# Token norms of a two-block transformer forward: ScalarE scales the tokens, plain transposes, per-feature shift and scale at the emptying of the banks, a shorter reciprocal root

## The chip, the cores and the metric

The kernel runs on one core of a Trainium2 chip. The metric is the device time of one execution in microseconds (us), as the median of several runs. The engines of a core work side by side, each through its own list of instructions in order, and wait for each other by semaphores: TensorE (PE, matrix products, with its weight loads shown as PEld), VectorE (DVE), ScalarE (ACT), GpSimd (POOL) and SyncE (SP, which here only starts DMAs).

## The reference, cut to what matters

256 tokens of 1024 features pass through two blocks. Everything is float32. The norms are these:

```python
def rms_norm(x, g):
    return x * lax.rsqrt(jnp.mean(x * x, -1, keepdims=True) + 1e-6) * g

def layer_norm(x, g, b):
    mu = jnp.mean(x, -1, keepdims=True)
    var = jnp.mean(jnp.square(x - mu), -1, keepdims=True)
    return (x - mu) * lax.rsqrt(var + 1e-5) * g + b

def first_block(x, ...):
    x = even_layer(x, ...)      # x + (forgetting and dilated attention of rms_norm(x)) @ w_out
    x = odd_layer(x, ...)       # x + (retention of rms_norm(x), group norm by head) @ w_out
    return rms_norm(x, final_norm)

def second_block(x, ...):
    h = layer_norm(x, ln_in_g, ln_in_b)
    for l in range(2):
        m = hybrid_mixer(h, ...)                       # compressed, selected, window attention, convolution
        h = layer_norm(ALPHA * h + m, ln1_g[l], ln1_b[l])
        f = swiglu(h, ...) if l == 0 else moe_swiglu(h, ...)   # dense FFN; 8 experts, top 2
        h = layer_norm(ALPHA * h + f, ln2_g[l], ln2_b[l])
    return h
```

## The kernel before, in words

The residual stream `x` lies in SBUF as two token tiles of 128 tokens by 1024 features (tile 0 and tile 1). Each layer multiplies the normed tokens by weights. The operand of those products is `xT`, the normed tokens transposed (features on the partitions), held as two parts, a high and a low one (`xT_129` and `xT_130` in the rows). One product of float32 quality is made of three matmuls of such parts, `mm3` (L181 to L183). The weights stream from HBM through SP's DMA queue (L42) into five buffers `w_raw`; ScalarE splits off the high part `w_hi` (L56) and VectorE the low part `w_lo` (L58), into four buffers each.

A layer ends in `out_units`, whose results are added to `x`. The last four pairs of weight chunks are run for tile 0 first (48 matmuls of 128x512), then `done(0, ...)` is called, then the same 48 for tile 1. `done(tt, ...)` is the norm of one tile: add the result to `x`, statistics, reciprocal root, transposes into `xT`. The next layer opens with `token_units`: 72 matmuls of 128x256 that need only tile 0, then `late`, which is `done(1, ...)`, then 72 that need tile 1. So each norm of tile 0 has tile 1's 48 matmuls to lie beside, and each norm of tile 1 the next layer's 72 matmuls of tile 0 (ahead of the MoE layer there are none: its router needs the norm first). Where an instruction stands in its engine's list is decided when the program is built, by a scheduler that takes the instructions in the order of the code unless it reckons that another is ready earlier; PE then runs its list strictly in order.

The boundaries with such a norm are six: the setup at the start (both tiles, nothing beside it), even to odd layer (both with `rms`), odd layer to mixer 0, mixer 0 to FFN, FFN to mixer 1 and mixer 1 to MoE (all with `layer_norm`, in short LN). A last norm, with no transposes, writes the output.

Before, the factor r of a token (the reciprocal root) is put into the transposing matmul: `diagonal` writes r on the diagonal of a 128x128 matrix `dr` (L397), and the matmul of `x` with `dr` (L411, float32, 8 for a tile, recorded as 16 passes) transposes and scales at once. For LN, VectorE has before that written (y - mean) * g over `x` (L381, two instructions of 128x512), and the shift b comes from a matmul of 24 rows in bf16 ahead of each bank's transposes (L407, two for a tile). The bank is emptied in two pieces of 128x512 by ScalarE (L429, high part) and VectorE (L431, low part); with `rms`, in 8 pieces of 128x128 each, which also apply the scale by feature (L419, L423). `update` later completes `x` itself as x * r + b (L389 on VectorE; for the MoE layer ScalarE L386 and GpSimd L387). `rsqrt` (L311 to L321) is 9 small VectorE instructions for one variance: a first guess by integer arithmetic and three Newton steps of two.

```python
t.matmul(out, l[0], r[0], start=start, stop=False, skip_group_check=True)   # L181
...
self.nc.tensor.matmul(ps[:, k, :], src[:, d], dr[:], start=shift is None, stop=True,   # L411
```

Of the kernel before, what the change touches and what calls it, by code (L numbers as in the profile page):

```python
# [119 lines left out]
class Stack:  # L120
# [34 lines left out]
    def load_shifts(self):  # L155
        for g in range(2):
            for j in range(3):
                p = 64 * g + 8 * j
                self.nc.gpsimd.dma_start(self.xs[p:p + 8, 1, 0:256].rearrange("p (i f) -> p i f", i=2),
                                         self.a["shifts"][2 * g:2 * g + 2].rearrange("i c f -> c i f"))  # L160

    def split_shifts(self):

        v = self.nc.vector
        for g in range(2):
            r = slice(64 * g, 64 * g + 24)
            t, f = self.shifts[r].rearrange("p i f -> p (i f)"), self.xs[r, 1, 0:256]
            v.tensor_copy(self.chunk[r], self.pick[r, 0:8])
            for j in range(2):
                v.tensor_copy(t, f)  # L170
                v.scalar_tensor_tensor(f, t, self.pick[r, 8 + j:9 + j], f, op0=ALU.mult, op1=ALU.add)
            v.tensor_copy(t, f)

    def shift(self, i):
        r = slice(64 * (i // 2), 64 * (i // 2) + 24)
        return self.shifts[r, i % 2], self.chunk[r]

# [128 lines left out]
    def rsqrt(self, mul, eps, *var):  # L306

        v = self.nc.vector
        xyt = [[self.small(1, "rs_" + n) for n in "xyt"] for _ in var]
        for (x, y, t), a in zip(xyt, var):  # L310
            v.tensor_scalar(x[:], a, 0.5 * mul, 0.5 * eps, op0=ALU.mult, op1=ALU.add)  # L311
        for x, y, t in xyt:
            v.tensor_single_scalar(y[:].bitcast(I32), x[:].bitcast(I32), 1, op=ALU.logical_shift_right)
        for x, y, t in xyt:
            yi = y[:].bitcast(I32)
            v.tensor_scalar(yi, yi, -1, 0x5f3759df - (1 << 22) - (1 << 31), op0=ALU.mult, op1=ALU.add)
        for _ in range(3):
            for x, y, t in xyt:
                v.scalar_tensor_tensor(t[:], y[:], y[:], x[:], op0=ALU.mult, op1=ALU.mult)  # L319
            for x, y, t in xyt:  # L320
                v.scalar_tensor_tensor(y[:], t[:], 1.5, y[:], op0=ALU.subtract, op1=ALU.mult)  # L321
        return [y[:] for _, y, _ in xyt]
# [19 lines left out]
    def rms(self, g, accs, between=0):  # L342

        ds = []
# [8 lines left out]
        for (tt, _), r in zip(accs, ds):  # L353
            ins = self.transpose(tt, self.x[:, tt], r, scale=g)
        return ins

    def layer_norm(self, tt, g, b, bT=None, acc=None, rms=None):

# [14 lines left out]
        if rms is None:  # L373
            r, = self.rsqrt(1.0, 1e-5, mv[:, 1:2])
        else:
# [3 lines left out]
            r, = self.rsqrt(1.0, 0.0, mv[:, 1:2])  # L379
# [10 lines left out]
        if bT is None:  # L390
            return update()
# [1065 lines left out]
```

## Time and profile before

| | |
|---|---|
| median of 3 runs | 1412.96 us (1412.95 to 1418.4) |
| the profiled execution | 1414.13 us, span 1412.4 us, so 1.7 us lie around the span |
| mean granted clock of PE | 0.99 of full |
| busy share of the span | PE 97%, DVE 78%, ACT 59%, POOL 7% |
| moved from HBM | 298.79 MB, mean 212 GB/s |

PE is busy for nearly the whole span, so a reader looks first for the few places where it is not, and asks at each which engine's work ends last. The rows that a profile prints give a start, a duration, the engine, the line, and what an instruction writes and reads. Matmuls overlap in PE's pipeline, so what one costs is read from the distance between two starts, not from its duration.

### The profile page before, as it was taken

The page shows a single profiled execution, that of the slowest core. Times are in us where ns is not written, and L with a number is a line of the kernel's source. Part 1 is how long each engine was busy: PE and PEld are TensorE (multiplying, and loading weights), DVE is VectorE, ACT ScalarE, POOL GpSimd, SP SyncE. Part 2 cuts the span into 40 slices and gives each one's busy share as a digit, 9 for nine tenths or more (in the row PEclk, how much of TensorE's full clock was granted, in tenths as well). Part 3 has the DMA queues.
Part 4 walks back from the last instruction along what each step waited for, and adds up shares of the span by engine and source line. Part 5 has one row for each costly group of instructions (what it writes and reads, how often), then busy time and mean ns, then how long its engine had stood idle before and what let it go on. Part 6 is the DMA issues. An engine that isn't in the chain of part 4 may idle for free. (4 is left out here: it accounts for less than half of the span.)

```text
span 1412.4 us, 24934 instructions
## 1 busy us (share of the span) xinstructions
PE 1367.0 (97%) x9907; PEld 1268.7 (90%) x9907; DVE 1101.9 (78%) x2013; ACT 836.0 (59%) x1394; POOL 102.5 (7%) x141
## 2 busy tenths in 40 slices
PE   7999999999999999999999999998999999999994
PEld 7999999799999898979998798977999999999983
DVE  7867666577777679887655479978989989989987
ACT  7666666364545357634444247744777777777762
POOL 2000000000000100010000000013010110120110
PEclk9999999999999999999999999998999999999997
DMA  8644444354444365436555455324989889889882
GB/s 299 236 150 150 150 151 150 119 205 176 173 156 165 99 252 200 146 124 225 181 187 197 151 197 207 121 99 145 365 319 352 320 324 349 305 320 348 328 326 76
DMA packets 45389, 301.58 MB, mean 214 GB/s; under 512 B 6016, under 2 KB 6256, under 8 KB 10576
## 3 DMA queue, kind: packets, MB, share of 16 engines
q1 hardware_dynamic: 42192, 293.20, 56.3%
q0 software_dynamic: 2928, 6.69, 1.7%
q8 instruction: 80, 1.31, 0.4%
q14 instruction: 45, 0.37, 0.1%
q10 hardware_dynamic: 144, 0.01, 0.0%
HBM read 298.79 MB, written 1.05 MB: 212 GB/s over the span
## 5 line engine op out<-in xcount | busy, mean ns | idle before, releaser
L58 DVE TENSOR_TENSOR w_lo<-w_raw,w_hi 128x1024 fp32r<-128x1024 f32 x553 | 673.0, 1248 | 157.3 <-ACT w_hi L56 156.5
L56 ACT ACTIVATE w_hi<-w_raw 128x1024 fp32r<-128x1024 f32 x553 | 560.9, 1055 | 217.2 <-PE ps L183 103.6
L181 PE MATMUL ps<-xT,w_hi 128*128 128x256 f32 x1072 | 304.5, 284 | 0.0
L183 PE MATMUL ps<-xT,w_lo 128*128 128x256 f32 x1072 | 301.3, 281 | 0.0
L182 PE MATMUL ps<-xT,w_hi 128*128 128x256 f32 x1072 | 301.1, 281 | 0.0
L181 PEld LDWEIGHTS ps<-xT,w_hi 128*128 128x128 f32 x1072 | 201.9, 188 | 2.8 <-issue 2.6
L183 PEld LDWEIGHTS ps<-xT,w_lo 128*128 128x128 f32 x1072 | 202.0, 188 | 0.3 <-issue 0.3
L182 PEld LDWEIGHTS ps<-xT,w_hi 128*128 128x128 f32 x1072 | 202.0, 188 | 0.0
L182 PE MATMUL ps<-w_lo,xe 128*128 128x256 f32 x704 | 199.3, 283 | 1.2 <-DVE w_lo L58 1.1
L181 PE MATMUL ps<-w_hi,xe 128*128 128x256 f32 x704 | 198.9, 283 | 0.0
L183 PE MATMUL ps<-w_hi,xe 128*128 128x256 f32 x704 | 198.8, 282 | 0.0
L181 PE MATMUL ps<-w_hi,xT 128*128 128x256 f32 x528 | 148.5, 282 | 0.0
L182 PE MATMUL ps<-w_lo,xT 128*128 128x256 f32 x528 | 147.7, 280 | 0.0
L183 PE MATMUL ps<-w_hi,xT 128*128 128x256 f32 x528 | 146.6, 279 | 0.0
L182 PEld LDWEIGHTS ps<-w_lo,xe 128*128 128x128 f32 x704 | 132.5, 188 | 2.9 <-DVE w_lo L58 2.2
L181 PEld LDWEIGHTS ps<-w_hi,xe 128*128 128x128 f32 x704 | 132.9, 189 | 0.6
L183 PEld LDWEIGHTS ps<-w_hi,xe 128*128 128x128 f32 x704 | 132.6, 188 | 0.0
L181 PEld LDWEIGHTS ps<-w_hi,xT 128*128 128x128 f32 x528 | 99.9, 189 | 0.3
L182 PEld LDWEIGHTS ps<-w_lo,xT 128*128 128x128 f32 x528 | 99.8, 189 | 0.3
L183 PEld LDWEIGHTS ps<-w_hi,xT 128*128 128x128 f32 x528 | 99.0, 188 | 0.1
L1232 POOL TENSOR_TENSOR x<-x,part 128x512 f32<-128x512 f32 x28 | 47.3, 1722 | 335.7 <-ACT part L1228 274.7
L465 ACT ACTIVATE P<-P,sm_mx 128x128 f32<-128x128 f32 (+1 forms) x128 | 56.9, 446 | 23.4 <-DVE sm_mx L461 23.1
(358 smaller groups left out, 2176.5 us busy)
## 6 DMA issues: line engine op xcount, KB each, us to landing
w_raw<-in_wts SPq DMA_DIRECT2D x271, 1024.0 KB, 4.9
w_raw<-in_wth SPq DMA_DIRECT2D x11, 512.0 KB, 3.6
w_raw<-in_ln_g POOLq DMA_DIRECT2D x3, 512.0 KB, 4.2
w_raw<-in_ln_b POOLq DMA_DIRECT2D x3, 512.0 KB, 5.4
x<-in_x SPq DMA_DIRECT2D x4, 256.0 KB, 3.8
out<-x SPq DMA_DIRECT2D x4, 256.0 KB, 2.1
dec<-in_dec POOLq DMA_DIRECT2D x1, 512.0 KB, 9.0
w_raw<-in_final_norm POOLq DMA_DIRECT2D x1, 512.0 KB, 4.0
```

The source lines that it names most:

```text
L56: self.nc.scalar.activation(hi[:, d], t[:, d], AF.Copy)
L58: self.nc.vector.tensor_sub(lo[:, d], t[:, d], hi[:, d].bitcast(F32))
L181: t.matmul(out, l[0], r[0], start=start, stop=False, skip_group_check=True)
L182: t.matmul(out, l[0], r[1], start=False, stop=False, skip_group_check=True)
L183: t.matmul(out, l[1], r[0], start=False, stop=stop, skip_group_check=True)
L465: s.activation(p[:, h, :], p[:, h, :], AF.Exp, bias=mx[:, o + h:o + h + 1], scale=-1.0, accum_out=rs[:, o + h:o + h + 1])
L1232: nc.gpsimd.tensor_add(x, x, t[:])
```

## The change

The factor r no longer goes through the matmul. With `rms`, ScalarE writes x * r into a second buffer (two of 128x512 for a tile, `to`), with LN it writes (y - mean) * r over `x` (bias -mean * r, a new small VectorE instruction, `ln_mr`), and VectorE then multiplies by g (two of 128x512). The transposes are plain ones by the identity. The shift b by feature is added where the bank is emptied, which for LN too is now done in 8 pieces of 128x128 by ScalarE (bias) and 8 by VectorE. `update` has only b left to add. The matmuls of the shifts, the six DMAs that loaded them and the VectorE work that split them are gone; one DMA brings a table of them in float32. `rsqrt` still has 9 instructions for a variance, made another way (the guess in one, a step of four and a step of three), and takes two variances in one set, which the group norm of the odd layer uses.

```diff
-    def rsqrt(self, mul, eps, *var):
+    def rsqrt(self, mul, eps, var):
         v = self.nc.vector
...
+        x, y, t = (self.small(2, "rs_" + n)[:, 0:var.shape[1]] for n in "xyt")
+        k = (1024 / 27) ** 2
+        v.tensor_scalar(x, var, k * mul, k * eps, op0=ALU.mult, op1=ALU.add)
+        v.tensor_scalar(y.bitcast(I32), x.bitcast(I32), -0.5, float(0x5f3759df - (1 << 31)), op0=ALU.mult, op1=ALU.add)
+        v.tensor_mul(t, y, y)
+        v.tensor_mul(t, t, x)
+        v.scalar_tensor_tensor(t, t, 10 / 3, t, op0=ALU.subtract, op1=ALU.mult)
+        v.scalar_tensor_tensor(y, t, 5.0, y, op0=ALU.add, op1=ALU.mult)
+        v.tensor_mul(t, y, y)
+        v.tensor_mul(t, t, x)
+        self.last = v.scalar_tensor_tensor(y, t, 64 / 3, y, op0=ALU.subtract, op1=ALU.mult)
+        return y
...
-    def rms(self, g, accs, between=0):
+    def rms(self, g, accs, to, between=0):
...
-            r, = self.rsqrt(1.0 / D, 1e-6, ms[:])
-            ds.append(self.diagonal(r))
+            r = self.rsqrt(1.0 / D, 1e-6, ms[:])
+            for d in self.halves():
+                self.acted = self.nc.scalar.activation(to[:, tt, d], self.x[:, tt, d], AF.Copy, scale=r)
...
-            ins = self.transpose(tt, self.x[:, tt], r, scale=g)
+            ins = self.transpose(tt, to[:, tt], scale=g)
...
+        mr = self.small(1, "ln_mr")
+        v.scalar_tensor_tensor(mr[:], mv[:, 0:1], -1.0, r, op0=ALU.mult, op1=ALU.mult)
         for d in self.halves():
-            v.scalar_tensor_tensor(xs[:, d], y[:, d], mv[:, 0:1], g[:, d], op0=ALU.subtract, op1=ALU.mult)
+            self.acted = self.nc.scalar.activation(xs[:, d], y[:, d], AF.Identity, bias=mr[:], scale=r)
+        for d in self.halves():
+            self.last = v.tensor_mul(xs[:, d], xs[:, d], g[:, d])
         def update(spread=False):
             for d in self.halves():
-                if spread:
-                    self.nc.scalar.activation(xs[:, d], xs[:, d], AF.Copy, scale=r)
-                    self.nc.gpsimd.tensor_add(xs[:, d], xs[:, d], b[:, d])
-                else:
-                    v.scalar_tensor_tensor(xs[:, d], xs[:, d], r, b[:, d], op0=ALU.mult, op1=ALU.add)
+                (self.nc.gpsimd if spread else v).tensor_add(xs[:, d], xs[:, d], b[:, d])
...
-    def diagonal(self, r):
-        dr = self.sm.tile([128, 128], F32, name="dr", bufs=2)
-        self.last = self.nc.vector.tensor_scalar(dr[:], self.ident, r, None, op0=ALU.mult)
-        return dr
...
-            if shift is not None:
-                rows, chunk = shift
-                self.nc.tensor.matmul(ps[:], rows, chunk[:, 4 * n:4 * n + 4, None].to_broadcast([24, 4, 128]),
-                                      start=True, stop=False, skip_group_check=True)
             for k in range(4):
                 d = slice((4 * n + k) * 128, (4 * n + k + 1) * 128)
-                self.nc.tensor.matmul(ps[:, k, :], src[:, d], dr[:], start=shift is None, stop=True,
-                                      skip_group_check=True)
-            if scale is None:
-                ins = self.split_into(self.xT[0][:, 4 * n:4 * n + 4, t], self.xT[1][:, 4 * n:4 * n + 4, t], ps[:])
-                continue
+                self.nc.tensor.transpose(ps[:, k, :], src[:, d], self.ident)
             for k in range(4):
                 c = 4 * n + k
                 hi, lo = (x[:, c, t] for x in self.xT)
-                self.nc.scalar.activation(hi, ps[:, k], AF.Copy, scale=scale[:, c:c + 1])
+                if scale is None:
+                    self.nc.scalar.activation(hi, ps[:, k], AF.Identity, bias=shift[:, c:c + 1])
+                else:
+                    self.nc.scalar.activation(hi, ps[:, k], AF.Copy, scale=scale[:, c:c + 1])
             for k in range(4):
...
-                ins = self.nc.vector.scalar_tensor_tensor(lo, ps[:, k], scale[:, c:c + 1], hi.bitcast(F32), op0=ALU.mult,
+                f, op = (shift, ALU.add) if scale is None else (scale, ALU.mult)
+                ins = self.nc.vector.scalar_tensor_tensor(lo, ps[:, k], f[:, c:c + 1], hi.bitcast(F32), op0=op,
                                                           op1=ALU.subtract)
...
+        nc.gpsimd.dma_start(self.shifts[:], a["shifts"])
...
+            to = self.spare()
+            nc.gpsimd.memset(to[:, :, 0:1], 0.0)
```

The instructions also come to stand in other places. On PE, at the end of mixer 0, the list before runs as follows where tile 0's matmuls end and tile 1's begin (`ps` are the accumulators, `yc` and `q` the operands of the output product):

```order
L181 MATMUL ps_6985<-w_hi_6996,q0_5588 128x512
L182 MATMUL ps_6985<-w_lo_6997,q0_5588 128x512
L183 MATMUL ps_6985<-w_hi_6996,q1_5589 128x512
L407 LDWEIGHTS shifts_132
L407 MATMUL ps_7083<-chunk_131,shifts_132 128x512
L181 MATMUL ps_6986<-w_hi_6711,yc0_5586 128x512
L182 MATMUL ps_6986<-w_lo_6712,yc0_5586 128x512
L183 MATMUL ps_6986<-w_hi_6711,yc1_5587 128x512
```

`ps_6985` belongs to tile 0 and `ps_6986` to tile 1; between them stands only one matmul of the shifts. Then, after 21 matmuls of tile 1, the transposes of tile 0's norm:

```order
L181 MATMUL ps_6986<-w_hi_6854,yc0_5586 128x512
L182 MATMUL ps_6986<-w_lo_6855,yc0_5586 128x512
L183 MATMUL ps_6986<-w_hi_6854,yc1_5587 128x512
L411 MATMUL ps_7075<-dr_7073,x_111 128x128 x4
L411 MATMUL ps_7083<-dr_7073,x_111 128x128 x4
L181 MATMUL ps_6987<-w_hi_6854,yc0_5586 128x512
```

The list of the change at the same end of mixer 0 (`mm3` is L158 to L160 there, the transposes are L383, `cst` is the identity; `ps_6933` is tile 0's, `ps_6934` and `ps_6935` are tile 1's):

```order
L158 MATMUL ps_6933<-w_hi_6944,q0_5524 128x512
L159 MATMUL ps_6933<-w_lo_6945,q0_5524 128x512
L160 MATMUL ps_6933<-w_hi_6944,q1_5525 128x512
L383 MATMUL ps_7025<-cst_113,x_111 128x128 x4
L383 MATMUL ps_7038<-cst_113,x_111 128x128 x4
L158 MATMUL ps_6934<-w_hi_6659,yc0_5522 128x512
L159 MATMUL ps_6934<-w_lo_6660,yc0_5522 128x512
L160 MATMUL ps_6934<-w_hi_6659,yc1_5523 128x512
L158 MATMUL ps_6935<-w_hi_6659,yc0_5522 128x512
```

The transposes of tile 0 moved from behind 21 of tile 1's 48 matmuls to directly behind tile 0's last matmul, ahead of all 48. The end of mixer 1 reads the same: 5721 `mm3` matmuls of the program stood ahead of its first tile-0 transpose, and 5700 do now, of which the last is tile 0's last. At the other three boundaries the count moves by 2 to 4 matmuls only (even to odd 1697 to 1700, odd to mixer 0 3134 to 3136, FFN to mixer 1 5084 to 5088), and for tile 1's transposes not at all, at any of them.

On VectorE, the norm of tile 1 at the end of mixer 0 now stands like this, from its statistics on (`x` is the token tile, `ps` the transposes' bank, L368 the product with g, L372 the update, L395 the emptying):

```order
L294 SCALAR_TENSOR_TENSOR rs_y<-rs_t,rs_y 128x1
L295 TENSOR_TENSOR rs_t<-rs_y 128x1
L296 TENSOR_TENSOR rs_t<-rs_t,rs_x 128x1
L297 SCALAR_TENSOR_TENSOR rs_y<-rs_t,rs_y 128x1
L364 SCALAR_TENSOR_TENSOR ln_mr<-ln_mv,rs_y 128x1
L368 TENSOR_TENSOR x<-x,w_raw 128x512 x2
L372 TENSOR_TENSOR x<-x,w_raw 128x512 x2
L395 SCALAR_TENSOR_TENSOR xT_132<-ps,shifts,xT_131 128x128 x8
```

Before, the two `update` instructions (L389) alternated with the two that empty a bank (L431), one of each in turn; now both stand ahead of all eight pieces (L395).

## Rows read from the trace of the kernel before

**Rows 1.** The page's first part: busy time, share of the span, instructions of each engine.
```profile
PE 1367.0 (97%) x9907; PEld 1268.7 (90%) x9907; DVE 1101.9 (78%) x2013; ACT 836.0 (59%) x1394; POOL 102.5 (7%) x141
```
**Rows 2.** Waits of PE: total us, times, longest us.
```profile
PE ps L411 <- DVE dr L397: 13.8, 3, 8.9
```
**Rows 3.** Timeline of PE (start us, us, engine, line, op): transposes by either kind of matmul.
```profile
299.98 1.95 PE L411 MATMUL ps<-dr,x 128*128 128x128 f32 x16
301.69 0.37 PE L181 MATMUL ps<-w_hi,xT 128*128 128x256 f32 x1
...
1010.40 1.36 PE L1192 MATMUL ps<-cst,he 128*128 128x128 f32 x11
1011.52 0.37 PE L181 MATMUL ps<-w_hi,xe 128*128 128x256 f32 x1
```
**Rows 4.** Timeline, end of mixer 0: tile 0's last matmul to its transposes.
```profile
615.88 0.40 PE L183 MATMUL ps<-w_hi,q 128*128 128x512 f32 x1
...
616.53 0.50 PE L181 MATMUL ps<-w_hi,yc 128*128 128x512 f32 x1
...
616.87 0.39 PE L182 MATMUL ps<-w_lo,yc 128*128 128x512 f32 x1
617.10 0.39 PE L183 MATMUL ps<-w_hi,yc 128*128 128x512 f32 x1
...
617.77 0.21 DVE L372 BATCH_NORM_AGGREGATE ln_mv<-ln_st 128x2 f32<-128x12 f32 x1
...
621.54 1.95 PE L411 MATMUL ps<-dr,x 128*128 128x128 f32 x16
```
**Rows 5.** Timelines of ACT and DVE: pieces of the norms.
```profile
948.20 0.71 ACT L386 ACTIVATE x<-x,rs_y 128x512 f32<-128x512 f32 x1
...
498.58 1.28 DVE L367 TENSOR_TENSOR w_raw<-x,w_raw 128x512 f32<-128x512 f32 x2
...
301.08 2.18 ACT L419 ACTIVATE xT<-ps,scales 128x128 fp32r<-128x128 f32 x8 [5.33 <-PE ps L411]
...
302.25 2.16 DVE L423 SCALAR_TENSOR_TENSOR xT<-ps,scales,xT 128x128 fp32r<-128x128 f32 x8 [4.07 <-ACT xT L419]
...
295.97 0.15 DVE L311 TENSOR_SCALAR rs_x<-ms 128x1 f32<-128x1 f32 x1
296.16 0.15 DVE L313 TENSOR_SCALAR rs_y<-rs_x 128x1 int32<-128x1 int32 x1
```
**Rows 6.** Windows, odd layer to mixer 0: five engines' busy us, PEclk, DMA share, GB/s.
```profile
506.00:507.00 1.00, 1.00 (x7) 1.00 (x6) 0.93 (x2) 0.60 (x1) 0.00 (x0) 0.50 1.02 426
...
509.00:510.00 1.00, 1.00 (x10) 1.00 (x9) 1.00 (x2) 0.00 (x0) 0.00 (x0) 0.85 0.50 66
```
**Rows 7.** Timeline, end of mixer 0, tile 1: VectorE's add, PE's transposes, PE after them.
```profile
631.97 1.28 DVE L369 SCALAR_TENSOR_TENSOR x<-x,ps 128x512 f32<-128x512 f32 x2
...
638.13 0.38 PE L407 MATMUL ps<-chunk,shifts 24*128 24x512 bf16 x1
638.44 1.16 PE L411 MATMUL ps<-dr,x 128*128 128x128 f32 x8
...
640.76 0.37 PE L181 MATMUL ps<-w_hi,xT 128*128 128x256 f32 x1
```
**Rows 8.** Timeline, end of mixer 1, tile 1: statistics, the router's copy.
```profile
956.36 0.21 DVE L372 BATCH_NORM_AGGREGATE ln_mv<-ln_st 128x2 f32<-128x12 f32 x1
...
965.95 0.17 DVE L1069 COPY r_l<-ps 128x8 f32<-128x8 f32 x1 [1.03 <-PE ps L1112]
```
**Rows 9.** Timeline of PE, odd layer to mixer 0, tile 1's transposes.
```profile
504.87 2.88 PE L411 MATMUL ps<-dr,x 128*128 128x128 f32 x16 [2.10 <-DVE dr L397]
```
**Rows 10.** Timeline of the setup.
```profile
8.90 6.43 PE L411 MATMUL ps<-dr,x 128*128 128x128 f32 x32 [8.90 <-DVE dr L397]
...
9.87 2.00 ACT L56 ACTIVATE w_hi<-w_raw 128x1024 fp32r<-128x1024 f32 x2 [2.05 <-DMA w_raw<-in_wts]
10.10 0.29 DVE L397 TENSOR_SCALAR dr<-cst,rs_y 128x128 f32<-128x128 f32 x1
```

More of the change, by code (lines that the diff above doesn't have):

```diff
@@ L153, in rows @@
         return [t[:, i, :] for i in range(len(aps))]
[L155 to L176, printed above, removed]
     def mm3(self, out, l, r, start, stop):
@@ L352, in rms @@
             self.W.split(between)
-        for (tt, _), r in zip(accs, ds):
-            ins = self.transpose(tt, self.x[:, tt], r, scale=g)
+        for tt, _ in accs:
+            ins = self.transpose(tt, to[:, tt], scale=g)
         return ins
@@ L373, in layer_norm @@
         if rms is None:
-            r, = self.rsqrt(1.0, 1e-5, mv[:, 1:2])
+            r = self.rsqrt(1.0, 1e-5, mv[:, 1:2])
         else:
@@ L501, in setup @@
         self.xs = self.spare()
-        cst = c.tile([128, 210], F32, name="cst")
+        cst = c.tile([128, 200], F32, name="cst")
         self.scales = c.tile([128, 2, 8], F32, name="scales")
+        self.shifts = c.tile([128, 4, 8], F32, name="shifts")
+        nc.gpsimd.dma_start(self.shifts[:], a["shifts"])
         nc.scalar.dma_start(self.scales[:], a["scales"])
@@ L516, in setup @@
         self.cma, self.cmm = (cst[:, i:i + 32].rearrange("p (t n) -> p t n", t=2) for i in (136, 168))
-        self.pick = cst[:, 200:210]
         self.xT = [c.tile([128, 8, S], F32R, name=f"xT{i}") for i in range(2)]
-        self.chunk = c.tile([128, 8], BF, name="chunk")
-        self.shifts = c.tile([128, 2, 128], BF, name="shifts")
-        self.load_shifts()
         accs = [(tt, [self.bank([128, 512]) for _ in range(2)]) for tt in range(2)]
-        self.W.after = self.rms(self.scales[:, 0], accs, 1)
+        self.W.after = self.rms(self.scales[:, 0], accs, self.xs, 1)
         self.W.after_act = self.acted
@@ L549, in even @@
             self.setup()
-            def shifts():
-                yield
-                yield
-                with self.W.behind(self.W.after), self.W.behind(self.W.after_act):
-                    self.split_shifts()
-            self.pend.append(shifts())
             def fa_done(ps):
@@ L697, in retain @@
                 yn = io.tile([128, 2, 512], F32, name="yn")
-                mv = [self.small(2, "gn_mv") for _ in range(2)]
+                mv = self.sm.tile([128, 2, 2], F32, name="gn_mv")
                 for tt in range(2):
@@ L701, in retain @@
                     v.bn_stats(st6[:], o[tt][:])
-                    v.bn_aggr(mv[tt][:], st6[:])
-                rs = self.rsqrt(1.0, 1e-6, mv[0][:, 1:2], mv[1][:, 1:2])
-                for tt, r in enumerate(rs):
-                    mr = self.small(1, "gn_mr")
-                    v.scalar_tensor_tensor(mr[:], mv[tt][:, 0:1], -1.0, r, op0=ALU.mult, op1=ALU.mult)
-                    nc.scalar.activation(yn[:, tt, :], o[tt][:], AF.Identity, bias=mr[:], scale=r)
+                    v.bn_aggr(mv[:, tt, :], st6[:])
+                r, mr = self.rsqrt(1.0, 1e-6, mv[:, :, 1]), self.small(2, "gn_mr")
+                v.scalar_tensor_tensor(mr[:], mv[:, :, 0], -1.0, r, op0=ALU.mult, op1=ALU.mult)
+                for tt in range(2):
+                    nc.scalar.activation(yn[:, tt, :], o[tt][:], AF.Identity, bias=mr[:, tt:tt + 1], scale=r[:, tt:tt + 1])
                 yield
@@ L732, in odd @@
             gi, bi = self.rows(a["ln_in_g_2"], a["ln_in_b_2"])
-            bT = self.shift(0)
+            bT = self.shifts[:, 0]
             part = lambda c: [t[:, c, :] for t in y]
@@ L993, in mixer @@
                 g, b = self.rows(a["ln1_g_2"][l], a["ln1_b_2"][l])
-                bT = self.shift(1 + l)
+                bT = self.shifts[:, 1 + l]
                 bg(0)
@@ L1041, in ffn @@
             g, b = self.rows(a["ln2_g_2"][0], a["ln2_b_2"][0])
-            bT = self.shift(3)
+            bT = self.shifts[:, 3]
             part = lambda c: [t[:, c, :] for t in h]
@@ L1428, in layout @@
     c["cmp_w2_2"] = np.ascontiguousarray(i["cmp_w2_2"].reshape(2, 2, 2, 128, 64).transpose(0, 3, 1, 2, 4))
-    c["shifts"] = np.stack([i["ln_in_b_2"], i["ln1_b_2"][0], i["ln1_b_2"][1], i["ln2_b_2"][0]]).reshape(4, 8, 128)
+    c["shifts"] = np.stack([i["ln_in_b_2"], i["ln1_b_2"][0], i["ln1_b_2"][1], i["ln2_b_2"][0]]).reshape(4, 8, 128).transpose(2, 0, 1).copy()
     c["router"] = np.ascontiguousarray(i["moe_router_2"][0].reshape(8, 128, 8).transpose(1, 0, 2))
```

34 lines of the change are left out of this document (10 added, 24 removed).

## The prediction, made before the change was timed

> **What bounds the kernel now.** I read the busy shares first: PE 97%, VectorE 78%, ScalarE 59% [rows 1]. So nearly all time is PE's, and a change to the norms can act in two ways only: through the PE time of the transposes themselves, and through the few places where PE stands still for a norm. The list of PE's waits comes next: three waits for `dr` make 13.8 us, of which the longest, 8.9, is the start of the program [rows 2]. One of the others is at the odd layer's end, where PE waits 2.10 us for `dr` of tile 1 [rows 9]. Everywhere else the norm lies beside matmuls of the other tile. The end of mixer 0 shows how: tile 0's last matmul starts at 615.88, tile 1's first already at 616.53, and the chain of the norm (statistics at 617.77, `dr`, transposes at 621.54) runs meanwhile [rows 4]. The question to put to the change is whether that cover is still there.
>
> **What the change does, part by part.** All times are against the profiled execution, 1414.1 us.
>
> *Cheaper transposes.* 16 passes with `dr` take 301.69 - 299.98 = 1.71 us; 11 plain transposes take 1.12, so 8 take 0.82 [rows 3]. That saves 0.9 us for a tile. A shift matmul costs 0.31 (638.13 to 638.44 [rows 7]), two for each LN tile, so 0.6. Twelve tiles and eight LN tiles would give 12 x 0.9 + 8 x 0.6 = 15.6 us if PE never waited for the norm; that is the upper bound of the gain.
>
> *A longer chain.* VectorE's small instructions follow each other at 0.19 us (295.97 to 296.16 [rows 5]); nine of them are 1.7 us, and the scale -mean * r another 0.2. Then come ScalarE's pass over 512 features, 0.71, and VectorE's product with g, 0.64 each [rows 5], the second half one 0.7 later. Before, the nine ran between the two passes of VectorE, and only `dr` (0.3) followed. Emptying a bank goes from two passes of 512 to pieces: 8 on ScalarE take 2.18 and 8 on VectorE 2.16 [rows 5]. ScalarE and VectorE do more then, but neither is near its limit [rows 1]; what counts is where PE waits for them.
>
> *The end of mixer 0.* PE's new list has tile 0's transposes directly behind tile 0's last matmul, ahead of all 48 matmuls of tile 1, where before 21 of them came first. PE takes its list in order, so tile 1's matmuls, and behind them everything, wait for the chain. Statistics end at 617.98 [rows 4]; plus 1.7 + 0.2 is 619.9; plus 0.71 and 0.64 is 621.3 for the first half, 622.0 for the second; plus three passages between engines that I take at 0.06 each, and the last four transposes (0.4): tile 1's first matmul starts at 622.7 instead of 616.53 [rows 4], 6.2 us late. The work that hid the chain is no longer ahead of it. From that go the first shift matmul (0.3, counted in the 616.53) and the old transposes with the second shift, which stood inside tile 1's stretch (1.7 + 0.3). To it comes the clock.
>
> [...] So tile 1's matmuls end 6.2 - 0.3 - 1.7 + 1.9 = 6.1 us late. Then 72 matmuls of the next layer follow, tile 1's transposes save 0.9 and 0.6, and the first product with tile 1 waits longer than before: it needs the low part, and VectorE now has both updates (2 x 0.64 [rows 5]) ahead of the pieces, so some 1.6 us stand behind the transposes where 0.4 did (640.76 [rows 7]). I take +5.5 for this end. Lower bound +2.5: before, VectorE's add of tile 1 at 631.97 [rows 7] came two microseconds after PE had finished that tile, since the splits of the weights held VectorE, and if this time is what bounds, a stall of PE is partly absorbed. [...]
>
> *The end of mixer 1.* The same order and the same chain, so again +6.1 for the end of tile 1. There nothing lies beside tile 1's norm (statistics at 956.36, the router's copy at 965.95 [rows 8]), so the lateness goes on in full. The chain there is 0.9 longer and the transposes, which ran at half clock, save about 1.8. Sum +5.2, bounds +3 and +7.
>
> *The other three ends.* Their tile-0 transposes keep 21 or more matmuls of tile 1 ahead, moved by 2 to 4. Even to odd: PE bound on both tiles, 2 x 0.9, so -1.8 (bounds -1.8 and 0). Odd to mixer 0: tile 1's transposes already waited for the chain [rows 9]; the chain grows by about as much as the transposes shrink, tile 0 gives 1.5 but PE then only waits longer; -0.2 (-1.5 to +1.5). FFN to mixer 1: PE comes to tile 1's transposes earlier than before and stands some 2 us with perhaps a half clock behind it; +0.7 (-1.5 to +2).
>
> *The setup.* Before, PE works from 8.90, 6.43 us of it transposes [rows 10]. Now ScalarE's two passes over tile 1 stand ahead of the first split. They can't start before tile 1's r, which was there at 10.10 [rows 10], and end 2 x 0.71 later, at 11.5; so the split starts 1.6 us behind its 9.87 [rows 10], and with it the emptying of the banks, on which PE waits. PE itself is then no longer the late one, its 16 transposes taking half of the 32 passes. I take +1.3 (0, if PE's 6.43 us were the bound, to +2.7, if a half clock follows).
>
> *What costs nothing.* The group norm loses nine small instructions for each of four heads, 4 x 1.7 = 7 us of VectorE, in a stretch where PE is the bound; so 0. The six small DMAs and the splits of the shifts lay in the setup behind other work; 0. If that cover were gone, they would give up to 1 us back. The memset that claims `to` makes POOL take one weight buffer early; one load on SP's queue waits then for PE's use instead of VectorE's, some 6 us later, with 16 us to go before it is needed; 0, at the worst 2.
>
> Sum: 1.3 - 1.8 - 0.2 + 5.5 + 0.7 + 5.2 = +10.7, so 1424.8 against the profiled execution's 1414.1, and 1423.6 against the median of 1412.96.
>
> [...]
>
> **The rivals.**
> - *A. The stalls hold* as worked out: 1423.6, with bounds 1417 to 1430. For it: PE's list. Chance 0.63.
> - *B. Absorbed.* The place is the end of each mixer: VectorE's splits, not PE, bound tile 1's add (631.97 [rows 7]), the clock does not fall, and the stalls cost +3 each instead of 5.5 and 5.2; the sum is then 1.3 - 1.8 - 0.2 + 3 - 0.5 + 3 = +4.8 or less, 1413 to 1418: no change. It decides if tile 1's add stands before 634.5 in the new trace. Against it: at mixer 1 nothing lies behind to absorb. Chance 0.20.
> - *C. PE's saving counts in full.* If x * g were there when PE comes to the transposes, all 15.6 us would count: 1397. It needs the chain to take no longer than what PE still has ahead, which is nothing at the mixers: at least 5 us are missing twice. With the stalls of one mixer only it would be 1403. Chance 0.07.
> [...]
>
> **How the numbers follow.** 0.5% is 7 us, about what a measurement of this kernel tells from no change: slower begins at 1420.0, faster ends at 1405.9. Slower: nine tenths of A (0.57) and D (0.10), so 0.67. Same: B and the rest of A, 0.26. Faster: C, 0.07. The range goes from 1411, within B, to 1430, in the midst between A and D: it leaves out C and most of D, and a little of B. The likeliest case's own range is 1417 to 1430.
>
> **What would show it.** Right: PE waits for x (the product with g) of about 5 us at 616 to 622 and again at the end of mixer 1 (941 to 947), with tile 1's first matmul at about 6 us behind tile 0's last; then windows of 0.50 clock; 96 transposes at 0.10 and no matmul with 24 rows. Wrong in B: tile 1's matmuls late, but its add and the next layer's first product on time. Wrong in C: no wait ahead of the transposes at the mixers. [...] What would make the prediction wrong altogether is a chain much shorter than 4 us from statistics to transposes, or a wait that I saw no row for, such as ScalarE's splits standing ahead of its pass over the tokens.

## The result and the profile after

The changed kernel is slower: 1429.62 us (median of four runs, 1426.16 to 1430.58) against 1415.24 for the kernel before on the same chip (1412.95 to 1418.4), a ratio of 1.0103 [1.0087, 1.0119]. The prediction was 1423.6, slower, with a range of 1411 to 1430. The profiled execution took 1426.16 us with a span of 1424.4, 12.0 more than before's, so the trace below accounts for 12 of the 14.4 us between the medians.

The first part of the page, columns as in [rows 1]:
```profile
PE 1359.2 (95%) x9795; PEld 1264.5 (89%) x9795; DVE 1100.3 (77%) x2005; ACT 857.2 (60%) x1462; POOL 98.4 (7%) x137
```
PE has 112 matmuls less and is busy 7.8 us less than in [rows 1], while the span is 12 longer. So some 20 us are new idle time of PE. The list of PE's waits (total us, times, longest us) says where to look:
```profile
PE ps L383 <- DVE x L368: 20.5, 6, 5.3
PE ps L383 <- ACT w_raw L325: 8.6, 1, 8.6
PE ps L1049 <- POOL x L372: 2.5, 1, 2.5
```
The second row is the start of the program, which was in the 13.8 of [rows 2]. The first is new: the transposes (L383) wait for the product with g (L368), six times. The third is new as well. The timeline of the end of mixer 0 shows the longest wait (start us, us, engine, line, operation):
```profile
617.93 0.39 PE L160 MATMUL ps<-w_hi,q 128*128 128x512 f32 x1
...
619.81 0.21 DVE L349 BATCH_NORM_AGGREGATE ln_mv<-ln_st 128x2 f32<-128x12 f32 x1
...
621.78 0.16 DVE L364 SCALAR_TENSOR_TENSOR ln_mr<-ln_mv,rs_y 128x1 f32<-128x1 f32 x1
621.98 1.52 ACT L366 ACTIVATE x<-x,ln_mr,rs_y 128x512 f32<-128x512 f32 x2 [8.71 <-DVE ln_mr L364]
...
623.57 1.97 PE L383 MATMUL ps<-cst,x 128*128 128x128 f32 x8 [5.25 <-DVE x L368]
...
625.19 0.78 PE L158 MATMUL ps<-w_hi,yc 128*128 128x512 f32 x1
625.76 0.63 PE L159 MATMUL ps<-w_lo,yc 128*128 128x512 f32 x1
...
638.12 1.28 DVE L346 SCALAR_TENSOR_TENSOR x<-x,ps 128x512 f32<-128x512 f32 x2
```
Between tile 0's last matmul (617.93) and tile 1's first (625.19) lie 7.3 us; in [rows 4] they were 0.65 apart (615.88 and 616.53). Tile 1's add on VectorE comes at 638.12, in [rows 7] at 631.97. The transposes take 1.62 us for eight and the first two 128x512 matmuls stand 0.57 apart (0.34 in [rows 4]): that is half clock, as the windows of the same stretch show (busy us of PE, PEld, DVE, ACT, POOL, then granted clock, DMA share, GB/s):
```profile
620.00:621.00 1.00, 0.00 (x0) 0.00 (x0) 0.80 (x6) 0.00 (x0) 0.00 (x0) 0.75 0.00 0
621.00:622.00 1.00, 0.00 (x0) 0.00 (x0) 0.80 (x5) 0.02 (x1) 0.00 (x0) 0.50 0.00 0
...
625.00:626.00 1.00, 1.00 (x5) 0.90 (x4) 0.84 (x2) 1.00 (x6) 0.00 (x0) 0.50 0.00 0
...
627.00:628.00 1.00, 1.00 (x5) 0.83 (x4) 1.00 (x6) 0.00 (x0) 0.00 (x0) 0.83 0.00 0
628.00:629.00 1.00, 1.00 (x6) 0.81 (x5) 0.34 (x2) 0.00 (x0) 0.00 (x0) 1.00 0.00 0
```
The granted clock falls while PE stands still (0.75 in 620 to 621) and stays at 0.50 until 627 (0.83 in 627 to 628). The end of mixer 1 repeats this (0.50 from 951.6 to 958.4), and behind it the start of the MoE layer has its own new wait. Its timeline, tile 1's statistics to the router's copy:
```profile
969.70 0.21 DVE L349 BATCH_NORM_AGGREGATE ln_mv<-ln_st 128x2 f32<-128x12 f32 x1
...
973.46 1.97 PE L383 MATMUL ps<-cst,x 128*128 128x128 f32 x8 [3.57 <-DVE x L368]
...
974.66 2.48 POOL L372 TENSOR_TENSOR x<-x,w_raw 128x512 f32<-128x512 f32 x2 [16.86 <-PE ps L383]
974.81 1.19 DVE L1040 TENSOR_TENSOR r_c<-r_c,lower 128x64 f32<-128x64 f32 x1
...
976.04 1.19 DVE L1041 TENSOR_TENSOR r_c<-r_c,r_c 128x64 f32<-128x64 f32 x1
...
977.99 0.17 PE L1049 MATMUL ps<-r_selb,before 128*128 128x8 bf16 x1 [2.55 <-POOL x L372]
...
981.59 0.17 DVE L1033 COPY r_l<-ps 128x8 f32<-128x8 f32 x1 [1.64 <-PE ps L1076]
```
Before, the same two instructions on ranks took 0.23 us each, on the kernel before's own timeline:
```profile
960.57 0.23 DVE L1076 TENSOR_TENSOR r_c<-r_c,lower 128x64 f32<-128x64 f32 x1
960.83 0.23 DVE L1077 TENSOR_TENSOR r_c<-r_c,r_c 128x64 f32<-128x64 f32 x1
```
GpSimd's add now lies right over them, and each of the two, 1.19 us, lasts about as long as one of its two adds (2.48 us for both). PE is named as waiting for POOL, but its matmul reads what L1044 writes from the ranks, three instructions behind the second slow one. From statistics to copy it is 11.9 us, in [rows 8] 9.6.

To see where the 12 us come from, the n-th of the 8388 matmuls of `mm3` in one trace was set against the n-th in the other. The lateness is +0.1 us after the setup, and at the end of mixer 0 it goes from 2.1 to 8.7 at the stand, 9.6 behind the half clock, and back to 6.6 when tile 1 is through. At the end of mixer 1 it goes from 7.5 to 15.3, back to 13.4 and up to 15.6 at the start of the MoE layer; then it falls to 11.9. Between these steps it drifts: +1.9 in the body of the even layer, +1.7 in the odd, +0.7 in the mixers and the FFN together, and -3.6 in the MoE layer, though nothing was changed in their bodies.

### The profile page after: what moved, and what is told of

It is laid out like the page before. It is cut to its first block, busy times and chain, and to the rows that moved or that the text cites. A ratio compares the mean times of both kernels' runs of the same rounds, so it can differ in the third digit from the quotient of the medians.

```text
span 1424.4 us, 24779 instructions
## 1 busy us (share of the span) xinstructions
PE 1359.2 (95%) x9795; PEld 1264.5 (89%) x9795; DVE 1100.3 (77%) x2005; ACT 857.2 (60%) x1462; POOL 98.4 (7%) x137
## 5 line engine op out<-in xcount | busy, mean ns | idle before, releaser
L158 PE MATMUL ps<-xT,w_hi 128*128 128x256 f32 x1072 | 306.5, 286 | 0.0
L160 PE MATMUL ps<-xT,w_lo 128*128 128x256 f32 x1072 | 303.3, 283 | 0.0
L158 PEld LDWEIGHTS ps<-xT,w_hi 128*128 128x128 f32 x1072 | 205.2, 191 | 2.8 <-issue 2.6
L160 PEld LDWEIGHTS ps<-xT,w_lo 128*128 128x128 f32 x1072 | 205.2, 191 | 0.3 <-issue 0.3
L159 PEld LDWEIGHTS ps<-xT,w_hi 128*128 128x128 f32 x1072 | 205.2, 191 | 0.0
L158 PE MATMUL ps<-w_hi,xe 128*128 128x256 f32 x704 | 197.2, 280 | 0.0
L160 PE MATMUL ps<-w_hi,xe 128*128 128x256 f32 x704 | 196.4, 279 | 0.0
L158 PE MATMUL ps<-w_hi,xT 128*128 128x256 f32 x528 | 150.9, 286 | 0.6 <-ACT xT L390 0.6
L160 PE MATMUL ps<-w_hi,xT 128*128 128x256 f32 x528 | 148.9, 284 | 1.1 <-DVE xT L395 0.9
L158 PEld LDWEIGHTS ps<-w_hi,xe 128*128 128x128 f32 x704 | 132.5, 188 | 0.6
L160 PEld LDWEIGHTS ps<-w_hi,xe 128*128 128x128 f32 x704 | 132.4, 188 | 0.0
L158 PEld LDWEIGHTS ps<-w_hi,xT 128*128 128x128 f32 x528 | 102.3, 194 | 1.6 <-ACT xT L390 1.0
L160 PEld LDWEIGHTS ps<-w_hi,xT 128*128 128x128 f32 x528 | 101.0, 192 | 2.0 <-DVE xT L395 2.0
L437 ACT ACTIVATE P<-P,sm_mx 128x128 f32<-128x128 f32 (+1 forms) x128 | 56.9, 446 | 22.1 <-DVE sm_mx L433 21.9
```

The lines of the kernel that those rows point to most:

```text
L159: t.matmul(out, l[0], r[1], start=False, stop=False, skip_group_check=True)
L160: t.matmul(out, l[1], r[0], start=False, stop=stop, skip_group_check=True)
L437: s.activation(p[:, h, :], p[:, h, :], AF.Exp, bias=mx[:, o + h:o + h + 1], scale=-1.0, accum_out=rs[:, o + h:o + h + 1])
```

## The experiments

The theory behind the prediction: PE's list has tile 0's transposes ahead of tile 1's 48 matmuls at both mixers, and that order costs the time. Rivals: the chain or the sharing between VectorE and GpSimd at the MoE layer; and the drift, for which the new places of the tiles in SBUF were suspected. All ratios are against the kernel before on the same chip.

**The order undone in the change.** Tile 0's transposes are put behind 10 of tile 1's 16 groups of matmuls at the mixers, 30 matmuls. The splits of the next weights, which the program writes behind them, move along.
```diff
+                for i, m in enumerate(todo):
+                    mm(tt, *m)
+                    if tt and hold and i + 1 == hold:
+                        self.W.after = fin()
...
+        if hold:
+            return lambda: self.transpose(tt, xs, shift=bT)
```


> The changed kernel with one thing moved: at the ends of both mixers tile 0's transposes are emitted behind 30 of tile 1's 48 matmuls, not directly behind tile 0's last matmul. The norm itself is the same. If PE's stall ahead of these transposes is the cause (theory A): the two waits of about 5 us go, with the half clock behind them, and the time falls by 9 to 12 us, to about 1418. If the longer chain and the pieces at the emptying of the banks are the cause (theory B), or the pace of the matmuls elsewhere (theory C), the time falls by less than 4 us.

1420.78 us, 1.0040 [1.0025, 1.0054]: about 9 of the 14 us come back. In its trace the steps at the two mixers are +3.1 and +3.3, and what is left of them stands at tile 1's transposes, where PE now waits 3.28 us at mixer 0 and 6.37 at mixer 1. VectorE's and PE's rows of the timeline at mixer 1:
```profile
961.85 1.28 DVE L348 SCALAR_TENSOR_TENSOR x<-x,ps 128x512 f32<-128x512 f32 x2
...
968.13 1.97 PE L387 MATMUL ps<-cst,x 128*128 128x128 f32 x8 [6.37 <-DVE x L370]
```
Tile 1's add stands 2 us behind PE's last matmul of the tile (959.9), because the emptying of tile 0's banks (2.16 us from 957.51) and the splits behind it (2.35 us from 959.59) hold VectorE; PE then waits 6.37 us. A place behind 30 matmuls thus costs at the other end; behind 24 (below, at other addresses) the same steps are +0.3 and +1.3.

**The order alone, in the kernel before.** The old norms stay, and tile 1's matmuls at the mixers are put behind tile 0's transposes.
```diff
+                with self.W.behind(tt == 1 and early and self.turned):
+                    for w, pair in units[:-1]:
```


> The kernel before, with its old norm, and one thing moved: at the ends of both mixers tile 1's 48 matmuls stand behind tile 0's transposes. If the place on PE's list is the cause (theory A): two waits of about 5 us for the diagonal appear, with a half clock behind them, and the kernel is slower by 9 to 12 us, though nothing of the norm changed. If the new norm's chain and pieces are the cause (theory B), it stays within 3 us.

1427.05 us, 1.0088 [1.0071, 1.0105]. Its timeline of PE at the end of mixer 0, and two windows:
```profile
615.65 0.39 PE L408 MATMUL ps<-chunk,shifts 24*128 24x512 bf16 x1
620.77 3.63 PE L412 MATMUL ps<-dr,x 128*128 128x128 f32 x16 [4.74 <-DVE dr L398]
624.15 0.48 PE L181 MATMUL ps<-w_hi,yc 128*128 128x512 f32 x1
...
621.00:622.00 1.00, 1.00 (x6) 1.00 (x6) 0.00 (x0) 0.00 (x0) 0.00 (x0) 0.50 0.09 16
...
624.00:625.00 1.00, 1.00 (x7) 0.86 (x7) 0.80 (x2) 0.56 (x1) 0.00 (x0) 0.94 0.00 0
```
With neither the new chain nor the new transposes, the order makes PE stand for 4.74 us and costs 12.5 us in all (1427.05 - 1414.51), nearly what the change does. The clock is back in 624 to 625 (0.94), some 3.4 us after PE set in again at 620.77; in the change it was back in 627 to 628 (0.83), some 3.8 us after 623.57. These are two places, too few to tell more. The lateness grows by 6.4 us at each mixer here.

**The addresses.** The change removes `dr` and the shifts' tiles, narrows `cst` from 210 to 200 columns and adds a table, by which most later tiles move in SBUF. Here the change's program has the old addresses, by unused columns.
```diff
-        cst = c.tile([128, 200], F32, name="cst")
+        cst = c.tile([128, 210], F32, name="cst")
...
+        self.shifts = c.tile([128, 136], F32, name="shifts")[:, 0:32].rearrange("p (i c) -> p i c", i=4)
+        nc.gpsimd.memset(self.sm.tile([128, 232], F32, name="pad", bufs=1)[:, 0:1], 0.0)
```


> The changed kernel with the tiles of SBUF at the addresses that they had before (the table of constants padded, the table of shifts moved behind xT, an unused tile in the small pool); the instructions are otherwise the same, but for one memset. If the addresses set the pace of the matmuls (theory C): the 128x256 matmuls on xT go back from 0.120 to 0.1177 us apart, those on the experts' tokens from 0.117 to 0.1195; the first makes the layers up to mixer 1 about 7 us shorter, the second the MoE about 4 us longer, together -1 to -4 us. If the pace has another cause (a drift of this execution, the transfers), both stay as they are in the changed kernel, and the time within 1 us.

1427.33 us, 1.0087 [1.0070, 1.0104], not clearly different from the change. But two rows of the page (costliest groups: total us, mean ns), first of the kernel before, then of the change, then of this one, show that the addresses do act:
```profile
L182 PE MATMUL ps<-xT,w_hi 128*128 128x256 f32 x1072 | 301.1, 281 | 0.0
L182 PE MATMUL ps<-w_lo,xe 128*128 128x256 f32 x704 | 199.3, 283 | 1.2 <-DVE w_lo L58 1.1
```
```profile
L159 PE MATMUL ps<-xT,w_hi 128*128 128x256 f32 x1072 | 303.0, 283 | 0.0
L159 PE MATMUL ps<-w_lo,xe 128*128 128x256 f32 x704 | 197.0, 280 | 1.3 <-DVE w_lo L58 1.3
```
```profile
L159 PE MATMUL ps<-xT,w_hi 128*128 128x256 f32 x1072 | 301.1, 281 | 0.0
L159 PE MATMUL ps<-w_lo,xe 128*128 128x256 f32 x704 | 199.6, 283 | 1.3 <-DVE w_lo L58 1.1
```
In the change the matmuls with `xT` are slower and those with `xe` (the MoE layer's) faster; with the old addresses both go back. Summed over the durations of all groups of one kind, the old addresses give 8.2 us back on `xT` and take 6.9 on `xe` and 3.0 on the outputs' `y` and `h`. The lateness shows it best: against the kernel before, this trace drifts by 0.3 us in the bodies of all layers together, where the change drifts by +4.3 up to the MoE layer and by -3.6 in it. These two nearly cancel. With this pair (the change at old addresses against the kernel before) each boundary's step can be read without the drift; the section on the prediction uses them.

**GpSimd out of the MoE layer's start.** In the change, the update with b there goes to VectorE.
```diff
-            self.normalise(True)
+            self.normalise(False)
```


> The changed kernel with one thing changed: ahead of the MoE layer, VectorE and not GpSimd adds the shift to the tokens. If GpSimd's adds hold up VectorE's ranks of the router (two instructions of 64 columns took 1.19 us there instead of 0.23): the router's matmuls no longer wait 2.5 us, and the time falls by 2 to 4 us. If they only lie side by side and PE would wait for the pieces at the emptying of the bank anyway: within 1 us, or slower by up to 2.6 us, which is the adds' own time on VectorE.

1427.59 us, 1.0090 [1.0069, 1.0111]. VectorE's and PE's timeline there:
```profile
977.84 0.22 DVE L1040 TENSOR_TENSOR r_c<-r_c,lower 128x64 f32<-128x64 f32 x1
...
979.02 0.37 PE L1076 MATMUL ps<-routerp,xT 128*128 128x8 f32 x1 [1.03 <-DVE xT L395]
...
980.69 0.22 DVE L1041 TENSOR_TENSOR r_c<-r_c,r_c 128x64 f32<-128x64 f32 x1
```
The ranks take 0.22 again, so GpSimd's add was what stretched them. But the step at the MoE layer's start falls only from 2.3 to 1.4 us, since the updates now stand ahead of the pieces of `xT` and PE waits for those. The total does not tell this from no effect.

**GpSimd's add issued behind the ranks.** The second update's instruction is put behind the ranks' last in the order in which the program is written.
```diff
+            with self.W.behind(first if i else None):
+                f(spread)
```


> The changed kernel with GpSimd's add of tile 1 ahead of the MoE issued only after VectorE's ranks of tile 0. If the two engines hold each other up there: the ranks' two slow instructions fall from 1.19 to 0.23 us, PE's wait of 2.5 us in the midst of the router's matmuls to about 0.6, and the time by 1 to 2 us. If the add then holds up something else (the pieces at the emptying, ScalarE's pass over the tokens): within 1 us.

1429.99 us, 1.0105 [1.0090, 1.0120]. This run tells nothing: the edit changed a list and made no engine wait for another, so GpSimd started as early as before, in the two rows of its timeline, and the ranks were as slow:
```profile
978.98 2.49 POOL L373 TENSOR_TENSOR x<-x,w_raw 128x512 f32<-128x512 f32 x2 [17.12 <-PE ps L384]
979.14 1.19 DVE L1041 TENSOR_TENSOR r_c<-r_c,lower 128x64 f32<-128x64 f32 x1
```

**Parts of the change by themselves, in the kernel before.** First only the new `rsqrt` with the group norm that uses it; then only the new way at even to odd (ScalarE scales into `to`, plain transposes).
```diff
+            for d in self.halves():
+                self.acted = self.nc.scalar.activation(to[:, tt, d], self.x[:, tt, d], AF.Copy, scale=r)
+            ds.append(None)
...
+                if dr is None:
+                    self.nc.tensor.transpose(ps[:, k, :], src[:, d], self.ident)
+                    continue
```


> The kernel before with the new reciprocal root alone, the group norm's two variances in one set too. If VectorE's small instructions there are hidden behind PE, as the prediction has it: within 1.5 us. If the group norm's nine fewer instructions for each head count: 2 to 7 us faster.

> The kernel before with the new way at one boundary alone, even to odd layer: ScalarE scales the tokens, plain transposes. If PE's saving counts where PE is the bound and its list keeps its order: 1.2 to 2 us faster (16 passes of 0.107 us for 8 of 0.102, two tiles). If the longer chain eats it: within 0.5 us or slower.

The root: 1413.94 us, 0.9996 [0.9987, 1.0005]; it is hidden. Even to odd: 1413.57 us, 0.9992 [0.9983, 1.0001]. Its trace, which is that of its slowest run (1415.8), gains 0.9 us at that boundary, all of it at tile 0: at tile 1 PE waits 0.37 us for ScalarE's pass. It loses 1.7 at the start of the MoE layer, where its program is the kernel before's and the half clock lasts longer (17 us instead of 10.2).

**The change repaired.** Tile 0's transposes behind 8 groups (24 matmuls), tiles at the addresses of the kernel below that is padded by 32 bytes, and the list edit of above, which does nothing.


> The changed kernel with all repairs together: tile 0's transposes at the mixers behind 24 of tile 1's matmuls, GpSimd's add of tile 1 ahead of the MoE behind VectorE's ranks of tile 0, and the addresses as in the padded kernel before. If the stalls, the collision and the addresses are all there is (theories A and C together): 9 to 12 us from the stalls, 1 to 2 from the collision, 6 to 9 from the addresses, so near 1409, below the kernel before. If the longer chain of tile 1 and the pieces cost by themselves: above 1414.

1413.84 us, 0.9995 [0.9986, 1.0004]: the whole loss is gone, and no gain is left. Some 2 us of that are the addresses': the kernel before with those addresses took 1412.24 in the same set of runs, 1.6 less. Tile 0's transposes wait for nothing at either mixer; what tile 0 saves, PE waits again at tile 1, and this is the first row of its list of waits:
```profile
PE ps L388 <- DVE x L371: 12.6, 5, 4.3
```

**Addresses in the kernel before.** Pads of a few columns shift the tiles behind them, first by 32 bytes each, then by 96 and 32.
```diff
+        nc.gpsimd.memset(self.sm.tile([128, 24], F32, name="pad", bufs=1)[:, 0:1], 0.0)
...
+                if e + base == 0:
+                    nc.gpsimd.memset(io.tile([128, 8], F32, name="pad", bufs=1)[:, 0:1], 0.0)
```


> The kernel before with two unused tiles of 32 bytes that shift what follows them in SBUF, so that the operands of the layers' output products (y, q, yc, h) lie in the same half of a 64-byte line as the split weights, and the experts' tokens (xe) in the other half; no instruction is changed but for two memsets. If the halves set the pace (theory C, read from the changed kernel and from the run with the old addresses): 128x256 matmuls on xe go from 0.120 to 0.117 us apart, 128x512 matmuls on y and h from 0.234 to 0.230, those on xT stay at 0.117, and the time falls by 7 to 9 us. If it was another thing about the addresses (the absolute place, a neighbour's traffic): some or all stay, and the time within 2 us.

> The kernel before with unused tiles again, of 96 and 32 bytes a partition. The padded kernel before this one showed 128x512 matmuls faster (0.234 to 0.230) but those on xe no faster, so the halves of 64 bytes are not the rule. What all traces so far agree with goes by the place in a 128-byte line: 128x256 matmuls are fast (0.117) where the moving tokens lie 32 bytes behind the weights (xT before, xe in the changed kernel), 128x512 matmuls slow (0.234) where the stationary tokens lie so. Here xe lies 32 bytes behind the weights, y, h and yc 64 away. If this is the rule: xe at 0.117, y and h at 0.230, xT at 0.117, and 4 to 7 us faster than the kernel before. If not: xe stays at 0.120, and 1 to 2 us faster as the last padded kernel.

With 32 bytes: 1412.24 us, 0.9986 [0.9977, 0.9995]; the 512-wide matmuls with `y` and `h` got a little faster (L181 with `y` 398 ns on average instead of 400), those with `xe` stayed (L182 283 ns in both), so the guess that the place within 64 bytes decides is out. With 96 and 32: 1404.36 us, 0.9929 [0.9913, 0.9945], the fastest kernel of all, with not one instruction of the computation changed. The page's row for `xe`:
```profile
L182 PE MATMUL ps<-w_lo,xe 128*128 128x256 f32 x704 | 197.1, 280 | 1.3 <-DVE w_lo L58 1.1
```
Summed over the durations of the groups of one kind, matmuls with `xe` give 5.2 us, with `hT` 3.0, with `y` 1.8, with `h` 1.3; these 11.3 are about the 10.2 by which the span is shorter.

**Both together.** Pads meant to give the good addresses, with tile 0's norms in the new way (transposes behind 24 matmuls), tile 1's in the old, and the new even to odd; then the good addresses with the new even to odd alone.


> The addresses of the kernel with 96 and 32 bytes, and of the change what paid: tile 0's norms the new way (with their transposes at the mixers behind 24 of tile 1's matmuls), tile 1's norms the old way with their shorter chain, even to odd layer the new way for both. If tile 0's saving of some 1.9 us at each end passes to the end, and tile 1 loses nothing: 4 to 8 us below the kernel with the addresses alone. If VectorE's pieces, or the splits queued behind them, hold up tile 1's add instead: no faster than that kernel.

> The kernel before with the addresses of 96 and 32 bytes, and with the new way at the even to odd boundary (ScalarE scales, plain transposes), which alone gave 0.7 us, within its uncertainty. If both add up: 1404 or a little below, at 0.992 to 0.993 of the kernel before. If the addresses' 10 us was in part chance of that build or of the clock: above 1408.

The first: 1410.84 us, 0.9973 [0.9964, 0.9983], some 6 us worse than the addresses alone. At odd to mixer 0, VectorE's add of tile 1 in the kernel with the addresses alone, and in this one:
```profile
495.90 1.27 DVE L331 TENSOR_TENSOR x<-x,ps 128x512 f32<-128x512 f32 x2
```
```profile
499.28 1.28 DVE L333 TENSOR_TENSOR x<-x,ps 128x512 f32<-128x512 f32 x2
```
It is 3.4 us later: six splits of weights in a row, which start 3.4 us later behind tile 0's longer norm, stand ahead of it. But this explains little of the 6 us, since the two kernels don't have the same addresses after all. Set against each other by lateness, their boundaries differ by 1.9 us in sum and the bodies of their layers, where the instructions are the same, by 4.8; the page's row for `xT`, first with the addresses alone, then here:
```profile
L181 PE MATMUL ps<-xT,w_hi 128*128 128x256 f32 x1072 | 304.5, 284 | 0.0
L181 PE MATMUL ps<-xT,w_hi 128*128 128x256 f32 x1072 | 305.5, 285 | 0.0
```
What the norms of this program are worth at equal addresses was not measured. The second: 1405.06 us, 0.9932 [0.9920, 0.9944]; the addresses' gain comes again in another program, and the cheaper transposes add nothing that the total shows.

## Why the prediction was right, by its own steps

The verdict and the mechanism were right, and rival A is the one that came. The forecast was +10.7 us and the medians are 14.4 apart; 1429.62 lies 0.4 below the upper end of the range. The sizes by lateness, in us, with the old addresses, where the drift is out, and in the change's own trace:

| step | predicted | measured, old addresses | the change |
|---|---|---|---|
| setup | +1.3 | +0.3 | 0.0 |
| even to odd | -1.8 | -1.1 | -1.0 |
| odd to mixer 0 | -0.2 | +0.4 | -0.2 |
| mixer 0 to FFN | +5.5 | +4.5 | +4.2 |
| FFN to mixer 1 | +0.7 | +0.7 | +0.5 |
| mixer 1 to MoE | +5.2 | +8.8 | +7.7 |
| layers' bodies and end | 0 | +0.3 | +0.7 |
| sum | +10.7 | +13.8 | +11.9 |

The small steps can't be told from chance. Where a run left the program of a boundary as in the kernel before, its step should be 0: the start varied from -0.6 to +0.9, odd to mixer 0 was -1.5 where the half clock of [rows 6] was missing (the kernel before with the order changed at the mixers alone, with the same wait of 2.10 us), and the start of the MoE layer +1.7 where it was longer.

*The end of mixer 0.* Tile 1's first matmul was to start 6.2 us late; in the change's trace the lateness grew by 6.6 there. The chain from the end of the statistics to the first half was put at 3.3 us and took 3.6 (620.02 to the transposes at 623.57). The eight transposes ran at half clock, 1.62 us where I had counted full pace (0.82), and tile 1's first matmuls lost another 1.0 to the clock; that is 1.5 in all, where the sum has 1.9. No run shows that 1.9 behind a stand of 5 us: it was my estimate, from the stretch at 0.50 of [rows 6]. In its place the trace has a clock of 0.50 for 3.8 us behind the stand (623.57 to 627.34). The three passages between engines, which I took at 0.06 each without a row, are 0.04, 0.03 and 0.06 there (ScalarE at 621.98, VectorE at 622.82, PE at 623.57). Then 1.9 came back where the old transposes had stood, as forecast (0.3 + 1.7), and 1.5 at tile 1's own transposes, as forecast (0.9 + 0.6). The low part behind these cost 0.4, where I had left some 0.9. So the term came out smaller, with each part of it seen.

*The mis-sized term is mixer 1 to MoE.* It was put at +5.2 with an upper bound of +7 and measured +8.8. The stand itself was near what was forecast (+6.1 for the end of tile 1, measured +6.2 with the old addresses); what failed is the step that the chain there would be 0.9 longer and the transposes 1.8 shorter, -0.9 in sum, with nothing new behind them. In the change's trace, from statistics to the first expert matmul it is 22.1 us against 19.8: chain +0.2, transposes -1.8 as forecast (before, the 16 passes ran from 959.92 to 963.31 at a granted clock of 0.50 in 960 to 963), and +3.9 between them and the router's copy, where I had put nothing. There PE waits 2.55 us (0.45 before), since GpSimd, no longer held up by ScalarE's pass in `update`, adds b exactly while VectorE makes the ranks, and the router's matmuls then run at 0.21 apart instead of 0.11, which is 1.5 us for fifteen of them, at a granted clock of 0.50 in 980 to 981 where before it was 1.00 in 964 to 966. The windows of the change there:
```profile
975.00:976.00 1.00, 0.44 (x4) 0.34 (x2) 1.00 (x1) 1.00 (x5) 1.00 (x2) 0.50 0.00 0
980.00:981.00 1.00, 1.00 (x7) 1.00 (x6) 0.00 (x0) 0.78 (x2) 0.00 (x0) 0.50 1.06 451
...
989.00:990.00 1.00, 1.00 (x10) 1.00 (x10) 0.13 (x1) 0.46 (x2) 1.00 (x1) 0.93 0.00 0
```
Taking GpSimd out gave 0.9 back; that the half clock is the rest is read from the pace, not shown by a run, since nothing here could set the clock. Without the change, in the kernel with the new even to odd alone, the same place lost 1.7 where the half clock lasted 17 us instead of 10.2, so that much of the miss may be chance.

*What cost nothing.* The group norm and the root: shown by the run with the root alone. The moves of the other tile-0 transposes by two to four matmuls: no new wait of any size stands there. But even to odd gained 1.1 and not 1.8. In the trace of even to odd alone, tile 0 gives 1.1, a little more than the 0.9 forecast, and tile 1 nothing, since PE waits there for ScalarE's pass, 0.37 us ahead of the transposes and again between its two banks.

*The rivals.* B had its deciding point at tile 1's add before 634.5; it came at 638.12. C asked for no wait ahead of the transposes; there are two of 5 us. The chances and the range also count a D, with 0.10: a clock that stays low longer. No run shows what that would cost. What the runs show is this: a stretch of half clock stands at the FFN's end too (839.0 to 842.4), and at both mixers the stretches are 6.8 us long, where that of [rows 6] took 3.4, though 2.5 to 3.1 us of each lie in the stand and cost nothing. But the kernel with the new even to odd alone, which leaves the MoE layer's start as it was, shows 17 us at half clock there (958.6 to 975.6), and so does the kernel before with the pads of 96 and 32 bytes (953.0 to 970.1), where the kernel before itself shows 10.2 in two pieces; so its length differs for reasons that these runs don't show. At the setup the bound of +2.7 allowed for a half clock. The granted clock reads 1.00 there in both traces (8 to 16), while the passes stand 0.21 us apart in both, as the transposes at mixer 0 do at a granted clock of 0.50 (623.84 to 624.05), against 0.107 for those of [rows 3] (1.71 / 16); so these records can't settle it.

*What no step of mine held* is the drift: in the change the moved tiles cost 4.3 us up to the MoE layer (a little of that may be the half clock) and gave 3.6 there. That these two are of one size is luck, and without it the total would have come out less near.

*Open:* what about an address decides the pace. The pads of 96 and 32 bytes were chosen by the place within 128 bytes, and `xe`, `y` and `h` became faster as that rule said. But `hT` did too, of which it had said nothing, and in the kernel with both parts `xT`, for which the rule says 0.117, stood 0.119 apart (median). So the rule isn't shown. A form in which GpSimd's add really waits for the ranks wasn't tried.

## What to carry to other kernels

A cheaper instruction on the bound engine is worth nothing if its operand comes later than the engine's turn (here PE was busy 7.8 us less and the span was 12.0 longer): count how much independent work the new order leaves ahead of it, before counting the instruction. Where a scheduler or a list decides that order, the order alone can cost nearly as much as the whole change (12.5 of 14.4 us here), and putting it back is the first repair to try. When an edit adds or removes tiles, compare the pace of instructions that it didn't touch: a shift of all addresses can hide a loss or a gain of ten microseconds (pads alone gave 10.5 here), and is worth a sweep of its own.

## What the runs showed of the hardware

- The pace of the split matmuls changed with the places of their operands in SBUF: 128x256 matmuls with `xe` followed each other at 0.119 us (median) in the kernel before and at 0.117 in the change, those with `xT` at 0.117 before and 0.120 in the change, and 128x512 ones with `y` and `h` at 0.234 before and 0.229 in the change. With the old addresses put back into the change, the rows of `xT` and `xe` above went back from 283 to 281 ns and from 280 to 283. Pads of 96 and 32 bytes alone made the kernel before 0.7% faster (0.9929), with 280 ns for `xe` instead of 283.
- Two VectorE instructions of 128x64 on the ranks took 1.19 us each instead of 0.23 beside two GpSimd adds that took 2.48 us together, and 0.22 again with the adds on VectorE.
- At the end of mixer 0, the granted clock was 0.50 for 3.4 us around PE's wait of 4.74 us in the kernel before with the order changed, and for 6.8 us around one of 5.25 us in the change. After the same wait of 2.10 us at odd to mixer 0, behind the same instructions, it was 0.50 for 3.4 us in the kernel before (505.9 to 509.3); in the execution with the order changed at the mixers alone it did not fall, where the step was -1.5 us.
